# Gathers of three expert pairs in quarters, issued within the product with the third matrix, through bank g

## The chip, the core and the metric

The kernel runs on one core of one Trainium2 chip. TensorE (PE) multiplies into PSUM banks, VectorE (DVE) and ScalarE (ACT) read the banks and work on SBUF, and SyncE (SP) issues the DMAs. Each engine takes its own instructions in the order in which they stand; engines wait for each other by semaphores. The metric is the device time of one execution in microseconds, the median of several runs.

## The reference

Two layers of a backbone run for 128 context and 128 latent tokens, 256 in all, with 1024 features. What the change touches is the end of the second layer, a mixture of eight experts of which each token uses two:

```python
for e in range(N_EXPERTS):
    ye = jnp.matmul(jax.nn.silu(jnp.matmul(t, w1[e])) * jnp.matmul(t, w3[e]), w2[e])
    out = out + comb[:, e:e + 1] * ye
```

`w1` and `w3` are 1024 x 2816, `w2` is 2816 x 1024, all in 32-bit floats; `comb` is zero but for a token's two experts.

## The kernel before

**Numbers in two halves.** Every 32-bit operand is split into a high part (rounded to TensorE's fp32r) and a low part (the difference). A product is three matmuls: high x high, high x low, low x high. For weights, ScalarE casts the high part (`mwh`, line 1319) and VectorE subtracts for the low part (`mwl`, through `tt`, line 52). The tokens of an expert have `xh` and `xl`, the gated product has `gh` and `gl`.

**Pieces.** The generator `blocks` brings a weight matrix in pieces of 128 x 1024 numbers: two tiles along the contraction, 512 columns each. A piece costs one cast, one subtraction and six matmuls. Six buffers hold cast pieces (`mwh`, three in each of two pools), so a cast waits for the matmuls of the piece six places before. The loads (`mws`, `ws`, `vs`) go round a ring of larger buffers on SP's queue.

**Experts.** `experts` works through four pairs. Pair p2 holds experts 2 p2 and 2 p2 + 1. `gather` makes a selection matrix `sel` for the pair (`select`) and multiplies the 256 tokens (`hhh`, `hhl`) with it, so that each expert has its own tokens in at most 128 columns: 32 matmuls of 128 x 256 in four quarters, each quarter in one bank and two k tiles of the result; ScalarE copies `xh` from the bank (line 1387), VectorE makes `xl` (line 1388). Four transposes turn `sel` into `selT` through bank `g` (lines 1392 to 1394).

For an expert, each block of 512 columns of `w1` and `w3` gives two banks of 8 k tiles; then ScalarE applies SiLU (line 1448), VectorE multiplies, TensorE transposes the result through bank `g` (line 1452), and ScalarE and VectorE read `gh` and `gl` from there (lines 1455, 1456). The last block has 256 columns. Then the product with the third matrix, `w2`, runs in two halves of 512 columns over 22 k tiles; each half is scaled (`yh`, `yl`) and multiplied with `selT` into the accumulators `acc`.

**When the gather stands.** The first pair is gathered ahead of the experts. The others are gathered at line 1459, after the odd expert's products with `w1` and `w3` and ahead of its product with `w2`, all four quarters at once.

**PSUM.** Eight banks: three for `mm` (the products with weights, and before the change the gathers of the pairs behind the first), one for `g`, three and one for `acc`.

**The order.** The code is recorded, and a scheduler places each engine's instructions by its own estimate of when they can run, so neighbouring pieces of work interleave.

Of the kernel before, what the change touches and what calls it, by code (L numbers as in the profile page):

```python
# [7 lines left out]
F32 = mybir.dt.float32  # L8
# [4 lines left out]
ALU = mybir.AluOpType  # L13
# [11 lines left out]
KT = D // 128  # L25
# [16 lines left out]
def backbone(ctx, tc, x_prompt, x_sample, c, state_hgrn, state_mlstm_C, state_mlstm_n, state_mlstm_m,  # L42
# [5 lines left out]
    V, S, G, PE = nc.vector, nc.scalar, nc.gpsimd, nc.tensor  # L48
# [19 lines left out]
    ident = const.tile([128, 128], F32, name="ident")  # L68
# [30 lines left out]
    def bank(shape):  # L99
        return mmp.tile(shape, F32, tag="mm", name="mm", bufs=3)  # L100
# [961 lines left out]
    with ExitStack() as es:  # L1062
# [52 lines left out]
        for q4 in range(2):  # L1115
            banks = gemm_tm(ffn_w2[0], 512 * q4, 512, grhs, fbank, 1 + 3 * q4, spare)
# [33 lines left out]
    def gbank(shape):  # L1150
        return pe.tile(shape, F32, tag="g", name="g")
# [30 lines left out]
    z, _ = mix_out(1, mrhs, ms, ("e8",), obank, spare1, 2)  # L1182
# [53 lines left out]
    for tr in range(2):  # L1236
        for q4 in range(2):
            ps = bank([128, 4, 128])
# [5 lines left out]
            with tc.issue_after(last_act[0]):  # L1244
                behind = [S.copy(hh[:, tr, s], psf).ins]
# [109 lines left out]
    def experts(first_slot):  # L1355
# [5 lines left out]
        def gather(p2):  # L1361

            sel = firsts.pop() if firsts else select(p2, sl)
            xh = ms.tile([128, KT, 256], F32R, tag="e8", name="xh", bufs=2)
            xl = ms.tile([128, KT, 256], F32R, tag="e8", name="xl", bufs=2)
            rhs = [sel[:, tr].rearrange("p i t -> p (i t)") for tr in range(2)]
            def part(ps, k2, src, first, last):
                for k in range(2):
                    s = slice(128 * (k2 + k), 128 * (k2 + k) + 128)
                    for tr in range(2):  # L1370
                        mm(ps[:, k], src[:, tr, s], rhs[tr], first and k + tr == 0, last and tr == 1)

            banks = []
            if not first_slot and p2 == 0:
                banks = [pe.tile([128, 2, 256], F32, tag="acc", name="acc", bufs=3) for _ in range(3)]
                banks.append(adp.tile([128, 2, 256], F32, tag="ad", name="acc"))
                for k2, ps in zip(range(0, KT, 2), banks):
                    part(ps, k2, hh, True, False)
            for k2 in range(0, KT, 2):
                if banks:  # L1380
                    ps = banks[k2 // 2]
                else:
                    ps = bank([128, 2, 256])
                    part(ps, k2, hh, True, False)
                part(ps, k2, hl, False, True)
                o = slice(k2, k2 + 2)
                S.copy(xh[:, o], ps)
                done = V.tensor_tensor(xl[:, o], ps, xh[:, o].bitcast(F32), op=ALU.subtract).ins  # L1388
            ps = gbank([128, 2, 2, 128])
            for tr in range(2):  # L1390
                for i in range(2):
                    PE.transpose(ps[:, i, tr], sel[:, tr, i].bitcast(F32), ident)
            selT = ms.tile([128, 2, 2, 128], F32R, tag="selT", name="selT", bufs=2)
            S.copy(selT, ps)
            return sel, selT, xh, xl, done

        def slot_weights(p2, sel):
            pc = gbank([128, 2])
# [7 lines left out]

        nxt = gather(0)
        if not first_slot:
            with tc.issue_after(nxt[4]):
                V.tensor_reduce(most, pm, axis=AX.X, op=ALU.max)  # L1410
                V.tensor_copy(most_i, most)
            behind.append(nxt[4])
            late.append(nc.values_load(most_i[0:1, 0:1], min_val=0, max_val=256))
        for p2 in range(NE // 2):
            sel, selT, xh, xl, _ = nxt
            for i in range(2):
                e = 2 * p2 + i
                s = slice(128 * i, 128 * i + 128)
                gT = []
                if not first_slot and e in (2, 3):  # L1420
                    ng1 = ms.tile([128, 2, 512], F32, tag="vs", name="ng1")
                    o1 = slice(512 * (e - 2), 512 * (e - 2) + 512)
                    for j, ap in enumerate((ln1_g[1], ln1_b[1])):
                        nc.sync.dma_start(out=ng1[:, j], in_=bcast_row(ap[o1], 512))
                for f0 in range(0, DFF, 512):
                    n = min(512, DFF - f0)
                    b13 = []
                    for srcs in ([moe_w1[0, e]], [moe_w3[0, e]]) if n == 512 else ([moe_w1[0, e], moe_w3[0, e]],):
                        b = bank([128, 512])
                        for kt, wh, wl in blocks(srcs, KT, f0, n, ahead.pop(0) if ahead else ()):  # L1430
                            mm(b, xh[:, kt, s], wh, kt == 0, False)
                            mm(b, xl[:, kt, s], wh, False, False)
                            mm(b, xh[:, kt, s], wl, False, kt == KT - 1)
                        b13 += [b[:, c:c + n] for c in range(0, 512, n)]
                    if not first_slot and e == 0 and f0 == 0:
                        park(moe_w3[0, 0], (0, 2, 4, 6), 512)
                        park(moe_w1[0, 0], (0,), 1024)
                    if not first_slot and e in (2, 3) and f0 in (512, 1024):
                        tr = f0 // 1024
                        tt(x[:, tr, o1], x[:, tr, o1], ng1[:, 0], ALU.mult)  # L1440
                        tt(x[:, tr, o1], x[:, tr, o1], ng1[:, 1], ALU.add)
                    if not i and f0 == 1024:
                        if not first_slot and not p2:
                            with tc.issue_after(gated):
                                expert_weights()
                        cs = slot_weights(p2, sel)
                    t_ = wp.tile([128, n], F32, tag="wa", name="gt_", bufs=2)
                    act(t_, b13[0], AF.Silu)  # L1448
                    tt(t_, t_, b13[1], ALU.mult)
                    ps = gbank([128, n // 128, 128])  # L1450
                    for j in range(n // 128):
                        PE.transpose(ps[:, j], t_[:, j * 128:j * 128 + 128], ident)  # L1452
                    gh = ms.tile([128, n // 128, 128], F32R, tag="gh", name="gh", bufs=6)
                    gl = ms.tile([128, n // 128, 128], F32R, tag="gl", name="gl", bufs=6)
                    S.copy(gh, ps)
                    gated = V.tensor_tensor(gl, ps, gh.bitcast(F32), op=ALU.subtract).ins
                    gT += [(gh[:, j], gl[:, j]) for j in range(n // 128)]
                if i and p2 + 1 < NE // 2:
                    nxt = gather(p2 + 1)
                if e == NE - 1:  # L1460
                    out = ms.tile([128, 2, D], F32, tag="e8", name="out", bufs=2)
                for q4 in range(2):
                    o = slice(512 * q4, 512 * q4 + 512)
                    yb = bank([128, 512])
                    for kt, wh, wl in blocks([moe_w2[0, e]], 22, 512 * q4, 512):
                        gh, gl = gT[kt]
                        mm(yb, gh, wh, kt == 0, False)
                        mm(yb, gl, wh, False, False)
                        mm(yb, gh, wl, False, kt == 21)
                    if e == NE - 1 and q4:  # L1470
                        with tc.issue_after(loaded[0]):
                            gate = gate_rows(ms, "e8", 1, 1, 2)
                            ng = norm_rows(base, "p8", ln2_g[1], ln2_b[1])
                    yh = ms.tile([128, 512], F32R, tag="yh", name="yh", bufs=1)
                    yl = ms.tile([128, 512], F32R, tag="yl", name="yl", bufs=1)
                    act(yh, yb, AF.Copy, scale=cs[:, i:i + 1])
                    V.scalar_tensor_tensor(yl, yb, cs[:, i:i + 1], yh.bitcast(F32), op0=ALU.mult, op1=ALU.subtract)
                    if e == NE - 1 and q4:
                        for tr in range(2):
                            before_norm(tr, gate, out, 0)  # L1480
                    for tr in range(2):
                        new = not first_slot and e == 0
                        if new:
                            acc[tr, q4] = adp.tile([128, 512], F32, tag="ad", name="acc") if tr and q4 else abank()
                        mm(acc[tr, q4], selT[:, i, tr], yh, new, False)
                        mm(acc[tr, q4], selT[:, i, tr], yl, False, True)
# [46 lines left out]
```

## Time and profile before

| | |
|---|---|
| median of 3 runs | 1909.88 us (1909.39 to 1910.23) |
| profiled execution, its own time | 1913.11 us |
| span in its trace | 1911.4 us |
| TensorE busy | 1842.6 us, 96% |
| VectorE busy | 1473.4 us, 77% |
| ScalarE busy | 1187.9 us, 62% |
| HBM read | 493.45 MB |
| mean granted clock | 0.99 |

Durations are taken from the one profiled execution. A matmul's row tells a duration that overlaps with its neighbours; the pace is the distance from start to start. In rows of the order of time, equal instructions that follow each other are merged (x2, x4), and a bracket tells how long the engine had been idle and what ended it. The experts run from about 1085 us to the end.

### The profile page before, as it was taken

What the parts mean: (1) busy time and instruction counts of PE and PEld (TensorE: products, weight loads), DVE (VectorE), ACT (ScalarE), POOL (GpSimd) and SP (SyncE); (2) the same over time, 40 slices, a digit from 0 to 9 for tenths busy, and PEclk for the clock granted to TensorE, in tenths of its full rate; (3) what the DMA queues carried; (4) which work ended last, traced back from release to release, by engine and by line L of the source; (5) the groups of instructions that cost most, each with busy time, mean ns of one, the idle gap of its engine ahead of it and who ended that gap; (6) DMA issues with size and microseconds to landing.
All of it is one profiled execution on the core that took longest, in us unless ns stands there. A gap on an engine that the chain in (4) does not pass through costs nothing.

```text
span 1911.4 us, 30874 instructions
## 1 busy us (share of the span) xinstructions
PE 1842.6 (96%) x11846; PEld 1572.2 (82%) x11846; DVE 1473.4 (77%) x2179; ACT 1187.9 (62%) x1531; POOL 21.3 (1%) x51
## 2 busy tenths in 40 slices
PE   7999999998999899999999999999999999999996
PEld 4877889996998688788999787888887888788884
DVE  3587598676455658869957798989888898889887
ACT  4547555644444445665564587777776777677773
POOL 0000000000000000000000000000000000000000
PEclk9999999999999999999999999999999999999998
DMA  9866845567756585775555989999998999999993
GB/s 315 259 228 203 269 142 160 157 198 277 230 170 194 162 286 194 244 220 149 149 161 172 361 297 346 363 323 366 349 349 312 358 350 343 307 350 352 348 342 128
DMA packets 273579, 500.88 MB, mean 262 GB/s; under 512 B 17044, under 2 KB 56552, under 8 KB 273424
## 3 DMA queue, kind: packets, MB, share of 16 engines
q1 hardware_dynamic: 273424, 498.83, 78.0%
q8 instruction: 95, 1.56, 0.3%
q14 instruction: 60, 0.49, 0.1%
HBM read 493.45 MB, written 5.32 MB: 261 GB/s over the span
## 4 chain that ended last, share of the span: by engine, by line
PE 83%; DMA 9%; DVE 3%; ACT 2%; issue 1%; SPq 1%; DVEq 0%; ACTq 0%
PE mm L56 62%; PE fp L56 9%; DMA wa<-in_w_ada_dram 6%; PE adq L56 2%; PE pl L56 2%; PE acc L56 1%; PE pn L56 1%; DMA ws<-in_ffn_w_dram 1%; DVE wl L52 1%; PE g L1452 1%; DVE mwl L52 1%; PE pqk L56 1%; DMA ws<-in_w_in_dram 1%; PE po L56 1%; ACT wh L198 1%
## 5 line engine op out<-in xcount | busy, mean ns | idle before, releaser
L52 DVE TENSOR_TENSOR mwl<-mws,mwh 128x1024 fp32r<-128x1024 f32 x432 | 516.8, 1223 | 52.3 <-ACT mwh L1319 48.3
L1319 ACT CAST mwh<-mws 128x1024 fp32r<-128x1024 f32 x432 | 445.8, 1052 | 117.1 <-PE mm L56 109.1
L52 DVE TENSOR_TENSOR wl<-ws,wh 128x1024 fp32r<-128x1024 f32 (+1 forms) x275 | 331.4, 1207 | 189.9 <-ACT wh L198 184.8
L198 ACT CAST wh<-ws 128x1024 fp32r<-128x1024 f32 (+1 forms) x275 | 284.7, 1036 | 308.8 <-PE mm L56 149.1
L56 PE MATMUL mm<-hTh,wh 128*128 128x256 f32 x1024 | 293.8, 289 | 4.6 <-ACT wh L198 2.5
L56 PE MATMUL mm<-hTl,wh 128*128 128x256 f32 x1024 | 293.0, 287 | 1.7 <-DVE hTl L52 1.0
L56 PE MATMUL mm<-hTh,wl 128*128 128x256 f32 x1024 | 291.7, 288 | 2.4 <-DVE wl L52 2.4
L56 PE MATMUL mm<-mwh,xh 128*128 128x512 f32 x704 | 278.8, 396 | 0.0
L56 PE MATMUL mm<-mwl,xh 128*128 128x512 f32 x704 | 277.5, 399 | 0.9 <-DVE mwl L52 0.8
L56 PE MATMUL mm<-mwh,xl 128*128 128x512 f32 x704 | 278.4, 396 | 0.0
L56 PEld LDWEIGHTS mm<-hTh,wh 128*128 128x128 f32 x1024 | 196.4, 192 | 10.3 <-ACT wh L198 2.7
L56 PEld LDWEIGHTS mm<-hTh,wl 128*128 128x128 f32 x1024 | 195.3, 192 | 10.5 <-issue 5.1
L56 PEld LDWEIGHTS mm<-hTl,wh 128*128 128x128 f32 x1024 | 196.8, 192 | 8.6 <-issue 4.2
L56 PEld LDWEIGHTS mm<-mwl,xh 128*128 128x128 f32 x704 | 132.3, 188 | 32.3 <-DVE mwl L52 2.0
L56 PEld LDWEIGHTS mm<-mwh,xl 128*128 128x128 f32 x704 | 132.3, 188 | 31.8 <-DVE xl L1388 0.4
L56 PEld LDWEIGHTS mm<-mwh,xh 128*128 128x128 f32 x704 | 132.3, 188 | 30.0
L56 PE MATMUL mm<-mwh,gh 128*128 128x512 f32 x352 | 139.4, 397 | 1.5 <-ACT gt__12538 L1448 1.5
L56 PE MATMUL mm<-mwh,gl 128*128 128x512 f32 x352 | 139.4, 397 | 0.0
L56 PE MATMUL mm<-mwl,gh 128*128 128x512 f32 x352 | 138.8, 396 | 0.5 <-DVE mwl L52 0.5
L52 DVE TENSOR_TENSOR mwl<-ws,mwh 128x1024 fp32r<-128x1024 f32 x74 | 89.9, 1223 | 16.3 <-ACT mwh L1319 15.6
L56 PE MATMUL fp<-hTh,wh 128*128 128x256 f32 x352 | 100.7, 287 | 0.0
L56 PE MATMUL fp<-hTl,wh 128*128 128x256 f32 x352 | 100.1, 285 | 0.0
(600 smaller groups left out, 3119.4 us busy)
## 6 DMA issues: line engine op xcount, KB each, us to landing
mws<-in_moe_w_dram SPq DMA_DIRECT2D x202, 1024.0 KB
ws<-in_w_in_dram SPq DMA_DIRECT2D x160, 512.0 KB
wa<-in_w_ada_dram SPq DMA_DIRECT2D x96, 512.0 KB
ws<-in_moe_w_dram SPq DMA_DIRECT2D x70, 512.0 KB
ws<-in_ffn_w_dram SPq DMA_DIRECT2D x62, 512.0 KB
mws<-in_moe_w_dram SPq DMA_DIRECT2D x28, 512.0 KB
ws<-in_w_branch_a_dram SPq DMA_DIRECT2D x16, 512.0 KB
ws<-in_w_branch_b_dram SPq DMA_DIRECT2D x16, 512.0 KB
```

Source lines behind the costliest of these rows:

```text
L52: V.tensor_tensor(out, a, b, op=op)
L56: return PE.matmul(out, lhsT, rhs, start=start, stop=stop, skip_group_check=True, **kw).ins
L198: S.copy(hi, st)
L1319: S.copy(h, t_)
L1452: PE.transpose(ps[:, j], t_[:, j * 128:j * 128 + 128], ident)
```

## The change

`gather` no longer issues the quarters for the pairs behind the first. It builds `sel` and the tiles, and returns a list of five steps: four quarters, each with its copy and subtraction, and the transposes of `sel`. In the loop over the k tiles of the product with `w2`, a step is taken off the list at k tiles 4, 8, 12, 16 and 20 of the first half. The banks of these quarters come from `gbank` in place of `bank`. The first pair's steps are run at once, as before. The second pass of `experts`, behind a branch for an expert with over 128 tokens, has the same code, and all four of its pairs take a bank from `gbank`; it does not run with these inputs.

```diff
--- before.py
+++ after.py
@@ -1376,23 +1376,29 @@
                 banks.append(adp.tile([128, 2, 256], F32, tag="ad", name="acc"))
                 for k2, ps in zip(range(0, KT, 2), banks):
                     part(ps, k2, hh, True, False)
-            for k2 in range(0, KT, 2):
-                if banks:
-                    ps = banks[k2 // 2]
-                else:
-                    ps = bank([128, 2, 256])
+            def step(k2):
+                ps = banks[k2 // 2] if banks else gbank([128, 2, 256])
+                if not banks:
                     part(ps, k2, hh, True, False)
                 part(ps, k2, hl, False, True)
                 o = slice(k2, k2 + 2)
                 S.copy(xh[:, o], ps)
-                done = V.tensor_tensor(xl[:, o], ps, xh[:, o].bitcast(F32), op=ALU.subtract).ins
-            ps = gbank([128, 2, 2, 128])
-            for tr in range(2):
-                for i in range(2):
-                    PE.transpose(ps[:, i, tr], sel[:, tr, i].bitcast(F32), ident)
+                done[:] = [V.tensor_tensor(xl[:, o], ps, xh[:, o].bitcast(F32), op=ALU.subtract).ins]
+
+            def places():
+                ps = gbank([128, 2, 2, 128])
+                for tr in range(2):
+                    for i in range(2):
+                        PE.transpose(ps[:, i, tr], sel[:, tr, i].bitcast(F32), ident)
+                S.copy(selT, ps)
+
+            done = []
             selT = ms.tile([128, 2, 2, 128], F32R, tag="selT", name="selT", bufs=2)
-            S.copy(selT, ps)
-            return sel, selT, xh, xl, done
+            steps = [lambda k2=k2: step(k2) for k2 in range(0, KT, 2)] + [places]
+            if not p2:
+                while steps:
+                    steps.pop(0)()
+            return sel, selT, xh, xl, done, steps
 
         def slot_weights(p2, sel):
             pc = gbank([128, 2])
@@ -1406,13 +1412,13 @@
 
         nxt = gather(0)
         if not first_slot:
-            with tc.issue_after(nxt[4]):
+            with tc.issue_after(nxt[4][0]):
                 V.tensor_reduce(most, pm, axis=AX.X, op=ALU.max)
                 V.tensor_copy(most_i, most)
-            behind.append(nxt[4])
+            behind.append(nxt[4][0])
             late.append(nc.values_load(most_i[0:1, 0:1], min_val=0, max_val=256))
         for p2 in range(NE // 2):
-            sel, selT, xh, xl, _ = nxt
+            sel, selT, xh, xl, _, steps = nxt
             for i in range(2):
                 e = 2 * p2 + i
                 s = slice(128 * i, 128 * i + 128)
@@ -1457,12 +1463,15 @@
                     gT += [(gh[:, j], gl[:, j]) for j in range(n // 128)]
                 if i and p2 + 1 < NE // 2:
                     nxt = gather(p2 + 1)
+                    steps = nxt[5]
                 if e == NE - 1:
                     out = ms.tile([128, 2, D], F32, tag="e8", name="out", bufs=2)
                 for q4 in range(2):
                     o = slice(512 * q4, 512 * q4 + 512)
                     yb = bank([128, 512])
                     for kt, wh, wl in blocks([moe_w2[0, e]], 22, 512 * q4, 512):
+                        if steps and kt and kt % 4 == 0:
+                            steps.pop(0)()
                         gh, gl = gT[kt]
                         mm(yb, gh, wh, kt == 0, False)
                         mm(yb, gl, wh, False, False)
```

TensorE at the gather of the third pair, before. The names: `sel` with `hhh` and `hhl` is the gather, `g<-ident,gt` transposes the gated product, `mwh,gh` is the product with the third matrix.

```order
L56 MATMUL mm<-mwl,xh 128x512
L56 MATMUL mm<-sel,hhh 128x256 x4
L56 MATMUL mm<-sel,hhl 128x256 x4
L56 MATMUL mm<-sel,hhh 128x256 x4
L56 MATMUL mm<-sel,hhl 128x256 x4
L1452 MATMUL g<-ident,gt__15194 128x128 x2
L56 MATMUL mm<-mwh,gh 128x512
```

TensorE at the second quarter of the same pair, in the changed kernel:

```order
L56 MATMUL mm<-mwl,gh 128x512
L56 MATMUL g<-sel,hhh 128x256 x4
L56 MATMUL g<-sel,hhl 128x256 x4
L56 MATMUL mm<-mwl,gh 128x512
L56 MATMUL mm<-mwh,gh 128x512
```

The third and fourth quarter, which stood back to back ahead of the product with the third matrix, now stand apart within it, in bank g.

ScalarE around the same gather, before. `gh` reads the transposes of the gated product, `mwh` are the casts of weight pieces, `xh` the copies of the gather.

```order
L1455 CAST gh<-g 128x512
L1319 CAST mwh<-ws 128x1024
L1319 CAST mwh<-mws 128x1024 x2
L1387 CAST xh<-mm 128x512 x2
L1448 ACTIVATE gt__15194<-mm 128x256
L1319 CAST mwh<-ws 128x1024
L1387 CAST xh<-mm 128x512 x2
L1455 CAST gh<-g 128x256
```

ScalarE in the changed kernel, from the same last `gh` on:

```order
L1461 CAST gh<-g 128x256
L1319 CAST mwh<-mws 128x1024 x2
L1319 CAST mwh<-vs 128x1024
L1319 CAST mwh<-mws 128x1024 x2
L1385 CAST xh<-g 128x512
L1319 CAST mwh<-mws 128x1024 x4
L1485 ACTIVATE yh<-mm,cs 128x512
L1319 CAST mwh<-mws 128x1024
L1385 CAST xh<-g 128x512
```

The four copies of `xh` come singly now, each with four to five casts of weight pieces between it and the next, and the first five casts behind the last `gh`.

## Rows read from the trace of the kernel before

**Rows 1.** The page's slices, 40 equal parts of the span: TensorE's busy tenths.

```profile
PE   7999999998999899999999999999999999999996
```

**Rows 2.** Stretches in us: length, busy us (instructions) by engine, clock, DMA.

```profile
core 0: us, PE busy (x) PEld busy (x) DVE busy (x) ACT busy (x) POOL busy (x), PEclk, DMA share, GB/s
1185.00:1251.00 66.00, 66.00 (x293) 53.34 (x292) 60.02 (x56) 52.21 (x56) 0.00 (x0) 1.00 1.02 363
...
1458.23:1461.62 3.39, 3.39 (x17) 3.39 (x17) 2.66 (x4) 0.59 (x1) 0.00 (x0) 0.54 1.04 372
...
1662.44:1665.79 3.35, 3.35 (x16) 3.35 (x17) 3.35 (x5) 1.24 (x2) 0.00 (x0) 0.55 1.03 390
```

**Rows 3.** What TensorE waited for, 1240 to 1870 us: total, times, longest.

```profile
PE mm L56 <- DVE xl L1388: 7.3, 2, 3.6
PE mm L56 <- DVE mwl L52: 0.8, 2, 0.5
PE g L1452 <- DVE gt__15031 L52: 0.4, 1, 0.4
```

**Rows 4.** Order of time, third pair: start us, duration us, engine, line, operation.

```profile
1451.35 0.59 ACT L1455 CAST gh<-g 128x512 fp32r<-128x512 f32 x1 [3.49 <-PE g L1452]
...
1452.99 1.05 ACT L1319 CAST mwh<-ws 128x1024 fp32r<-128x1024 f32 x1 [1.05 <-PE mm L56]
...
1453.94 1.99 ACT L1319 CAST mwh<-mws 128x1024 fp32r<-128x1024 f32 x2
...
1454.19 0.40 PE L56 MATMUL mm<-mwl,xh 128*128 128x512 f32 x1
...
1455.83 1.06 ACT L1387 CAST xh<-mm 128x512 fp32r<-128x512 f32 x2
...
1457.48 1.28 DVE L1388 TENSOR_TENSOR xl<-mm,xh 128x512 fp32r<-128x512 f32 x2
...
1458.23 1.22 PE L56 MATMUL mm<-sel,hhh 128*128 128x256 f32 x4 [3.64 <-DVE xl L1388]
...
1461.62 0.38 PE L1452 MATMUL g<-ident,gt__15194 128*128 128x128 f32 x2
...
1461.76 0.48 PE L56 MATMUL mm<-mwh,gh 128*128 128x512 f32 x1
```

**Rows 5.** Order of time, fourth pair.

```profile
1654.94 0.60 PE L1452 MATMUL g<-ident,gt__16875 128*128 128x128 f32 x4
...
1655.58 0.59 ACT L1455 CAST gh<-g 128x512 fp32r<-128x512 f32 x1 [5.80 <-PE g L1452]
...
1657.15 2.36 DVE L52 TENSOR_TENSOR mwl<-mws,mwh 128x1024 fp32r<-128x1024 f32 x2 [0.26 <-ACT mwh L1319]
...
1658.42 0.40 PE L56 MATMUL mm<-mwl,xh 128*128 128x512 f32 x1
...
1662.44 0.99 PE L56 MATMUL mm<-sel,hhh 128*128 128x256 f32 x4 [3.62 <-DVE xl L1388]
...
1665.79 0.56 PE L1452 MATMUL g<-ident,gt__16934 128*128 128x128 f32 x2
...
1666.43 0.40 PE L56 MATMUL mm<-mwh,gl 128*128 128x512 f32 x1
...
1666.66 0.40 PE L56 MATMUL mm<-mwl,gh 128*128 128x512 f32 x1
```

**Rows 6.** Order of time, second pair, TensorE.

```profile
1252.88 0.63 PE L56 MATMUL mm<-sel,hhl 128*128 128x256 f32 x4
...
1253.81 0.63 PE L56 MATMUL mm<-sel,hhl 128*128 128x256 f32 x4
...
1254.62 0.74 PE L56 MATMUL mm<-sel,hhh 128*128 128x256 f32 x4 [0.19 <-DVE gt__13440 L52]
...
1255.20 0.64 PE L56 MATMUL mm<-sel,hhl 128*128 128x256 f32 x4
```

**Rows 7.** DMA of the stretch 1085 to 1870 us.

```profile
DMA packets 143936, 268.04 MB, mean 341 GB/s; under 512 B 5133, under 2 KB 21517, under 8 KB 143886
```

## The prediction, made before the changed kernel ran

> **What bounds the kernel now.** I began with the page's slices [rows 1]: from the 24th on, where the experts run, TensorE is busy nine tenths or more in every slice but the last. A table of stretches sharpens this [rows 2]: between 1185 and 1251 us TensorE is busy all 66.00 us, VectorE 60.02 and ScalarE 52.21, at 363 GB/s. So TensorE sets the pace there, and VectorE runs at 91% beside it. The list of what TensorE waited for between 1240 and 1870 us is short [rows 3]: 7.3 us in two waits for xl, the low half of the gathered tokens; then 0.8 us in two for weight pieces and 0.4 in one at the bank g. No DMA heads it.
>
> The two xl waits are the gathers of the third and fourth pair. The order in time shows how one arises [rows 4]. ScalarE has stood 3.49 us for the transposes of the gated product and reads them at 1451.35. Then it casts three pieces (one at 1452.99, two from 1453.94) before it reaches xh at 1455.83, and VectorE reaches xl at 1457.48. TensorE's next work is the third quarter of the gather, which needs one of the three mm banks, and that is free only once xl is made. Its last product before the wait starts at 1454.19 and takes 0.23 us of pace, so it stands from 1454.42 to 1458.23: 3.81 us. The product with the third matrix stands behind the waiting quarter, and its pieces are cast meanwhile. Then comes a second loss: from 1458.23 to 1461.62 the granted clock averages 0.54 [rows 2], so most of the sixteen gather products run at 1.2 GHz in place of 2.4. The fourth pair repeats both [rows 5]: its last product starts at 1658.42, so it is idle from 1658.65 to 1662.44, 3.79 us, and then has a stretch at 0.55.
>
> **What the change removes.** Full pace for gather products is read from the second pair, where eight of them take from 1252.88 to 1253.81 [rows 6]: 0.93 us, so sixteen take 1.86.
> Third pair: idle 3.81, and half clock 3.39 - 1.86 = 1.53.
> Fourth pair: idle 3.79, and half clock 3.35 - 1.86 = 1.49. Two transposes and the first product behind them are slow too: 0.64 us (1665.79 to 1666.43) against 0.14 + 0.23 in the third pair, where the clock is back (1461.62 to 1461.76) [rows 4, 5]; 0.27 more.
> Second pair: the clock does not drop, but its third quarter starts at 1254.62 where 1253.81 + 0.47 would do, 0.34 us late, and its first four products take 0.58 in place of 0.47, 0.11 more [rows 6].
> Together 3.81 + 1.53 + 3.79 + 1.76 + 0.45 = 11.3 us, if nothing new waits.
>
> **What it adds and moves.** Nothing is computed more or less: a pair keeps 32 products and four transposes on TensorE, four casts and four subtractions behind them. SP issues the same DMAs; of two ws loads that stood together some now have a larger load between them. No wait of TensorE for a DMA stands in [rows 3], so I take zero for that, with rival C as its other end. The moved parts have three prices.
>
> First, each quarter now goes through the single bank g, so a quarter may wait for the xl of the one before, and the first for the gl of the last transposes. In the new order 22 to 34 other products lie between two quarters (three pairs), 5.1 to 7.8 us. ScalarE's cast of a quarter stands about five pieces further on in its queue than the quarter on TensorE. There are six buffers for cast pieces, so when the quarter ends ScalarE is at most one cast of about 1.05 us short of it. Then 0.6 for xh, VectorE's 1.2 for the piece ahead (two take 2.36 in [rows 5]), 0.7 for xl: some 3.5 us after the quarter, before 5.1 have passed. I take zero; what hides it is the product with the third matrix. Without that cover a quarter pays at least its own emptying, which I estimate at 0.59 + 0.69 = 1.28 us from the halves of the paired rows of xh (1.06) and xl (1.28) and a little for the hand-over.
>
> Second, ScalarE's wait for the gated product's transposes does not go away. Of the last full column block, in the new order they stand 2.7 pieces ahead of the first piece that ScalarE has not cast by then in the third pair, and 1.7 in the fourth. That piece is late next. With the rows of the fourth pair, counted from the transposes at 1654.94: gh begins 0.64 later, VectorE starts on the piece at 2.21 (1657.15) and ends it at 3.4. TensorE wants its low half after the transposes (0.36), 1.7 pieces of six products (2.35) and two products more (0.47), at 3.2. So 0.2 to 0.3 us of wait in the fourth pair; in the third it is wanted at 4.6, no wait. VectorE then gains about 0.2 us a piece. In the experts behind, the new order has three places with 2.0 pieces between; there it is wanted at 3.6, nearly level. I put 0.8 us for all of these. The bounds: nothing, since the old order shows 0.8 us of waits for pieces in all [rows 3]; and the two waits of 3.8 come back whole, which is rival A.
>
> Third, the last quarter is issued late, in the fourth pair two pieces into the next expert's first product, which needs its xl for the seventh of eight k tiles. Counted from the end of that product's first piece, VectorE is done after some 3.6 us, and TensorE wants it after 1.4 (second piece) + 0.93 (the quarter) + 1.4 (third) + 0.23 = 4.0. Close but covered: zero, at most 0.5.
>
> Sum: 11.3 - 0.8 = 10.5 us. The profiled execution took 1913.11 us, its span 1911.4 and 1.7 around it; so 1902.6 in its terms. It lay 3.2 us above the median of the three runs, 1909.88, and from that median I forecast 1899.4 us. Lowest: all 11.3 and the 1.2 of other waits gone, 1897.4, and about 1 us for the measurement.
>
> **The rivals.** A. The stall moves. Its root in the rows is ScalarE's wait for the transposes (3.49 us, and 5.80 in the fourth pair [rows 5]), not the gather. If TensorE waits for a low piece where it waited for xl, the idle comes back: half of it gives about 1905, all of it with the clock 1909. For it: the new order keeps these waits of ScalarE and brings more like them in the later experts. Against it: counted in the old orders, TensorE stood with two pieces of the next product already cast in the third pair, and without the gather it would have gone on; my count leaves 1 us of room there.
>
> B. Slower: one bank for everything. If ScalarE or VectorE come to the quarters late, TensorE waits at each with the weight products behind it. Twelve quarters at 1.28 us are 15.4 us, which gives 1899.4 + 15.4 = 1914.8. It decides from 11.3 / 12 = 0.94 us a quarter. Against it: transposes pass through g all along, and in 630 us TensorE waited once there, 0.4 us, for its input and not for the bank [rows 3].
> The Trainium skill (Perfetto Trace Analysis, Matmuls) says that independent groups of products should rotate through different PSUM banks, so that ScalarE and VectorE empty one while the next is filled; the change does the reverse with the quarters. By that rule the 15.4 us would be paid. The trace does not decide it: rotation over three banks did not spare the 7.3 us, and no row has gather products in a single bank.
>
> C. No gain: weights cannot come faster. From 1085 to 1870 us 268.04 MB move, at 341 GB/s [rows 7]; 11 us less needs 268.04 / 774 = 346. The 363 GB/s over 66 us [rows 2] speaks against it. It would leave the time near 1909.
>
> **How the numbers follow.** Forecast 0.73 (its own range 1896.5 to 1903), A 0.15, B 0.08, C 0.04. The range of 8 in 10 goes into A: 1896 to 1907. A measurement of this kernel tells 0.2% from no change, so faster means under 1906.1: the forecast and a third of A, 0.78. The same is the rest of A and C, 0.14. Slower is B, 0.08.
>
> **What would show it.** Right: in the list of TensorE's waits the line for xl is gone or under 1 us; the granted clock is 1.00 in every stretch from 1085 us to the end of the last expert; each quarter of eight products takes about 0.93 us; ScalarE still waits for the transposes of the gated product, without TensorE standing. A: waits of TensorE for low pieces, of 1 us and more, just behind the transposes of the last full column block. B: a dozen waits of products into g for xl. C: casts that wait for a DMA.

## The result, and the profile after

The changed kernel takes 1903.03 us, the median of five runs (1901.91 to 1904.31), against 1910.23 for five runs of the kernel before (1909.39 to 1916.76). The ratio is 0.9948, with a 95% interval of 0.9931 to 0.9965: faster by about half a per cent. Its profiled execution took 1904.31 us with a span of 1902.6, against 1913.11 and 1911.4.

TensorE's waits between 1240 and 1862 us in the changed kernel, the stretch that answers to 1240 to 1870 in [rows 3], by engine, what was waited for, total, times and longest:

```profile
PE mm L56 <- DVE mwl L52: 2.1, 5, 0.6
PE g L1458 <- DVE gt__15031 L52: 0.4, 1, 0.4
```

Against [rows 3], the 7.3 us for xl are gone, and the waits for low pieces have grown from 0.8 to 2.1 us. (One more, of 0.5 us, stands behind both stretches, at 1880.38 before and at 1871.61 in the changed kernel.) No quarter waits at bank g.

The stretches of the third and fourth pair in the changed kernel (columns as in [rows 2]):

```profile
1435.00:1490.00 55.00, 54.52 (x254) 44.62 (x253) 50.21 (x49) 39.20 (x46) 0.00 (x0) 1.00 0.98 349
1640.00:1700.00 60.00, 59.90 (x279) 48.77 (x278) 51.02 (x51) 42.75 (x51) 0.00 (x0) 1.00 0.99 359
```

The granted clock, 0.54 and 0.55 behind the stalls in [rows 2], is 1.00 in both, and 1.00 on average from 1085 to 1885 us. The order in time of the third pair, against [rows 4]:

```profile
1449.71 0.60 PE L1458 MATMUL g<-ident,gt__15135 128*128 128x128 f32 x4
...
1450.35 0.59 ACT L1461 CAST gh<-g 128x512 fp32r<-128x512 f32 x1 [3.51 <-PE g L1458]
...
1452.48 0.40 PE L56 MATMUL mm<-mwh,gh 128*128 128x512 f32 x1
...
1461.09 0.64 PE L56 MATMUL g<-sel,hhh 128*128 128x256 f32 x4
1461.56 0.63 PE L56 MATMUL g<-sel,hhl 128*128 128x256 f32 x4
...
1469.49 0.63 PE L56 MATMUL g<-sel,hhh 128*128 128x256 f32 x4
```

ScalarE still stands 3.5 us for the transposes, as before. But at 1452.48, 2.8 us after the transposes, TensorE is in the product with the third matrix, and the first quarter comes 8.6 us later, at 1461.09, and runs at full pace: four products in 0.47 us, as in [rows 6]. No bracket stands behind its rows: it waited for nothing.

To compare executions without what happens ahead of the experts, I take the time from the start of the first weight product of the experts to the start of the last. In the changed kernel these rows are:

```profile
1089.56 0.66 PE L56 MATMUL mm<-mwh,xh 128*128 128x512 f32 x2
...
1884.55 0.40 PE L56 MATMUL mm<-mwl,gh 128*128 128x512 f32 x1
```

794.99 us. In the kernel before the same two start at 1089.17 and 1893.31: 804.14 us. The change gains 9.15 us here. Following every 66th product through both traces tells where: 0.5 us at the second pair, 5.4 at the third, 5.1 at the fourth, 10.9 in all; then 1.8 us are given back in the last two experts.

One thing shows without a run. Take the kernel before and change one word, `bank` to `gbank` where the gather takes its bank, without the steps and the loop: the order of its instructions on TensorE, VectorE, ScalarE and SyncE is the same as the changed kernel's. So with bank g the steps at k tiles 4 to 20, the most visible part of the diff, place nothing; the scheduler spreads the quarters as soon as their bank is g. As built, the change is its bank.

### The profile page after: what moved, and what is told of

Same layout as the page of the kernel before. It is cut to its first block, busy times and chain, and to the rows that moved or that the text cites. A ratio compares the mean times of both kernels' runs of the same rounds, so it can differ in the third digit from the quotient of the medians.

```text
span 1902.6 us, 30784 instructions
## 1 busy us (share of the span) xinstructions
PE 1841.9 (97%) x11846; PEld 1570.5 (83%) x11846; DVE 1466.1 (77%) x2179; ACT 1177.5 (62%) x1531; POOL 21.2 (1%) x51
## 4 chain that ended last, share of the span: by engine, by line
PE 85%; DMA 9%; DVE 3%; ACT 1%; issue 1%; SPq 1%; DVEq 0%; ACTq 0%
PE mm L56 63%; PE fp L56 9%; DMA wa<-in_w_ada_dram 6%; PE adq L56 2%; PE pl L56 2%; PE acc L56 1%; PE g L56 1%; PE pn L56 1%; DVE mwl L52 1%; PE g L1458 1%; DMA ws<-in_w_in_dram 1%; DVE wl L52 1%; DMA ws<-in_ffn_w_dram 1%; PE pqk L56 1%; PE po L56 1%
## 5 line engine op out<-in xcount | busy, mean ns | idle before, releaser
L1319 ACT CAST mwh<-mws 128x1024 fp32r<-128x1024 f32 x432 | 437.4, 1051 | 83.0 <-PE mm L56 75.8
L56 PE MATMUL fp<-hTh,wl 128*128 128x256 f32 x352 | 100.2, 285 | 0.0
```

The source lines that it names most:

```text
L56: return PE.matmul(out, lhsT, rhs, start=start, stop=stop, skip_group_check=True, **kw).ins
L1319: S.copy(h, t_)
```

## The experiments

All times between the first and the last weight product are the rows above, read in each run's own trace. Each ratio is against runs of the kernel before that were made beside it: their median is 1914.32 us for e0, e1, e5 and e6, and 1912.63 for e7, e11 and e12. The times in the expectations go by about 1910 us for the kernel before, so it is the ratio that can be compared.

| run | first weight product starts | last starts | between | against before |
|---|---|---|---|---|
| before | 1089.17 | 1893.31 | 804.14 | |
| the change | 1089.56 | 1884.55 | 794.99 | -9.15 |
| before again (e0) | 1091.86 | 1896.11 | 804.25 | +0.11 |
| quarters in mm (e1) | 1092.90 | 1888.76 | 795.86 | -8.28 |
| third quarter in g (e5) | 1094.42 | 1898.64 | 804.22 | +0.08 |
| last two in g (e6) | 1092.44 | 1898.78 | 806.34 | +2.20 |
| last three in g (e7) | 1094.20 | 1889.19 | 794.99 | -9.15 |
| four in g, one behind the other (e11) | 1086.46 | 1916.02 | 829.56 | +25.42 |
| g in the third pair alone (e12) | 1088.28 | 1887.07 | 798.79 | -5.35 |

**e0, the kernel before again.**

> The kernel before, unchanged, profiled once more, since its profiled execution lay 3.2 us above its median. If that belongs to the stalls (the clock drops in some executions and not in others), the new profile's idle at the third and fourth pair is again about 3.6 us each and the time follows the number of drops, 1.5 us each. If it lies elsewhere, the experts take the same time as in the first profile to within 0.5 us and the difference stands ahead of them.

Median 1915.39 us, the ratio to its own kind 1.0013 (0.9999 to 1.0026). Between the weight products it took 804.25 us, 0.11 more than in the first profile, with the same two waits of 3.6 us; but the first weight product started 2.69 us later. So what differs between these two executions lies ahead of the experts. Over the nine traces that start lies between 1086.46 and 1094.42 us, and the change touches nothing there. A median of five runs carries this scatter; the column "between" does not.

**e1, the change with the quarters in mm.**

```diff
-                ps = banks[k2 // 2] if banks else gbank([128, 2, 256])
+                ps = banks[k2 // 2] if banks else bank([128, 2, 256])
```

> The changed kernel with its quarters back in the three mm banks; the steps stay in the product with the third matrix. In its order the third quarter of the third and fourth pair stands four to five pieces behind the transposes it used to follow, with pieces of the third product ahead of it. Theory (the stall is the third quarter standing ahead of that product while its bank is busy): the two waits for xl are gone here too, 1902 to 1905 us, ratio to before 0.994 to 0.997. Rival (the bank g is what does it): the waits of 3.6 us and the half clock come back, 1908 to 1911 us.

1905.12 us, ratio 0.9954 (0.9938 to 0.997). TensorE's waits from 1075 us on:

```profile
PE mm L56 <- DVE mwl L52: 3.0, 7, 0.6
PE mm L56 <- ACT gt__12538 L1454: 1.5, 1, 1.5
PE g L1458 <- DVE gt__15031 L52: 0.4, 1, 0.4
```

No line for xl. Bank g is not needed for the gain: here the steps in the loop do what the bank did. The first quarter of the third pair starts at 1456.21, behind the first matmul of the third product at 1455.74, so that product has its mm bank before any quarter takes one. The gain is 0.9 us smaller, with one more wait for a low piece (0.48 us at 1530.22) and one of the transposes ahead of it (0.31).

**e5, the third quarter alone in g.**

```diff
-                    ps = bank([128, 2, 256])
+                    ps = gbank([128, 2, 256]) if k2 == 4 else bank([128, 2, 256])
```

> The kernel before, with only the third quarter of each later pair in bank g; the others stay in mm and in their place. In its order the fourth quarter now stands where the third stood and takes the bank that the third took. Theory (a quarter ahead of the third product waits for a bank that xl frees): two waits of about 3.6 us for xl and both drops of the clock remain, 1908 to 1911 us. Rival (four banks for four quarters are enough): no wait, about 1900.

1913.09 us, ratio 0.9996 (0.9982 to 1.001), and 7.3 us in two waits for xl as before. Four banks do not help while the next user of mm stands ahead of the product.

**e6, the last two quarters in g.** As e5 with `k2 > 2`.

> The kernel before, with the third and fourth quarter of each later pair in bank g and the first two in mm. In its order the first two stay ahead of the third product and the last two stand some eight pieces into it; the order of the later experts is the old one. Theory: no wait for xl, clock 1.00, and none of the new waits for low pieces that the changed kernel has in its last two experts: 1898 to 1901 us, 1 to 3 us below the changed kernel. Rival (the new waits belong to the gather, not to the order of the later experts): like the changed kernel, 1902 to 1904.

1913.44 us, ratio 0.9992 (0.9976 to 1.0008): my theory failed, and so did its rival. Only the first two quarters stand ahead of the third product, and the stall is there whole:

```profile
1457.38 0.40 PE L56 MATMUL mm<-mwl,xh 128*128 128x512 f32 x1
...
1459.03 1.06 ACT L1387 CAST xh<-mm 128x512 fp32r<-128x512 f32 x2
...
1460.69 1.28 DVE L1388 TENSOR_TENSOR xl<-mm,xh 128x512 fp32r<-128x512 f32 x2
...
1461.42 0.80 PE L56 MATMUL mm<-mwh,gh 128*128 128x512 f32 x1 [3.64 <-DVE xl L1388]
```

Now the product itself (`mwh,gh`) waits 3.64 us for xl. Its sum needs an mm bank as well, and two of the three hold quarters; it starts when the first xl is made. It is 2.2 us slower than before. Behind the stall the weight products start 0.43 us apart in place of 0.23, and the stretch from 1461.40 to 1469.00 has a mean granted clock of 0.59 over 7.6 us:

```profile
1461.40:1469.00 7.60, 7.58 (x21) 5.97 (x21) 4.48 (x5) 2.59 (x3) 0.00 (x0) 0.59 0.76 279
```

**e7, the first quarter in mm, three in g.** As e5 with `k2 > 0`. The theory was mended for it: not a waiting quarter, but whatever next needs an mm bank.

> The kernel before, with the first quarter of each later pair in mm and the other three in bank g. In its order the first quarter stands ahead of the third product, the others 8 to 23 pieces into it. Theory as the runs so far leave it (what stalls is the next user of an mm bank, be it a quarter or the third product, when two of the three banks hold quarters whose xl stands behind three casts): with one quarter in mm a bank is left for the product, no wait for xl, 8 to 10 us less between the first weight product and the last than before. Rival (any quarter ahead of the product stalls it): the waits of 3.6 us remain and the gain is under 2 us.

1901.78 us, ratio 0.9934 (0.9908 to 0.996), 9.15 us less between the products, as much as the change. Its waits from 1240 us on:

```profile
PE mm L56 <- DVE mwl L52: 2.6, 6, 0.6
PE g L1452 <- DVE gt__15031 L52: 0.4, 1, 0.4
```

One quarter ahead of the product is harmless. Two stall it where ScalarE reaches their copies late. The second pair shows the other case: in the kernel before it too has its quarters in mm, but there ScalarE copies the first one right behind gh, with no cast of a weight piece between, and the wait behind is 0.19 us [rows 6], not 3.6:

```profile
1253.16 0.58 ACT L1455 CAST gh<-g 128x512 fp32r<-128x512 f32 x1
1253.63 0.60 ACT L1387 CAST xh<-mm 128x512 fp32r<-128x512 f32 x1
```

**e11, four quarters in g, nothing between.** The product's first matmul is held until the last quarter is issued; the rest as the kernel before.

```diff
...
-                    ps = bank([128, 2, 256])
+                    ps = gbank([128, 2, 256])
...
-                        mm(yb, gh, wh, kt == 0, False)
+                        with tc.issue_after(ahead_of.pop()) if ahead_of else nullcontext():
+                            mm(yb, gh, wh, kt == 0, False)
```

> The kernel before, with all quarters of the later pairs in bank g and the third product held back until the last quarter is issued, so that the four quarters follow each other on TensorE with nothing between. This is what the rule on rotating banks speaks of. Theory (bank g costs nothing only because the product fills the time of emptying): each quarter but the last waits for xh and xl of its own bank, 1.3 to 1.5 us, three a pair, besides the backlog of casts and the clock; 10 to 25 us longer than before. Rival (one bank is no price at all): the same time as before or less.

1939.96 us, ratio 1.0145 (1.0119 to 1.0171), 25.4 us more between the products, just over the 10 to 25 expected. Its waits, and one quarter's emptying with the start of the next:

```profile
PE g L56 <- DVE xl L1388: 12.6, 9, 1.4
PE g L1454 <- DVE gl L1458: 8.2, 3, 2.9
PE g L56 <- DVE gl L1458: 2.8, 3, 0.9
```

```profile
1467.67 0.59 ACT L1387 CAST xh<-g 128x512 fp32r<-128x512 f32 x1 [2.61 <-PE g L56]
1468.28 0.69 DVE L1388 TENSOR_TENSOR xl<-g,xh 128x512 fp32r<-128x512 f32 x1 [2.77 <-ACT xh L1387]
...
1469.03 1.22 PE L56 MATMUL g<-sel,hhh 128*128 128x256 f32 x4 [1.40 <-DVE xl L1388]
```

Each quarter but the first waits 1.40 us for the emptying of the one before (0.59 + 0.69 and the hand-over), nine times. The other 11.0 us of waits are of the last transposes and of each pair's first quarter, for the gl that empties the same bank ahead of them. The clock falls with the waits: 0.64 between 1461 and 1478 us. The Trainium skill (Perfetto Trace Analysis, Matmuls) says that independent groups should rotate through different PSUM banks, so that the emptying of one overlaps the matmuls of the next; with one bank and nothing between, nothing overlaps, and the trace agrees with it. In the change the same single bank costs nothing: 22 to 34 weight products lie between two quarters of a pair, and no quarter waits.

**e12, bank g in the third pair alone.** As e5 with `p2 == 2`.

> The kernel before, with bank g for the quarters of the third pair alone. Two things are told apart. Gain: the wait of 3.6 us and the half clock of the third pair are gone, 5.3 us, and those of the fourth remain. New waits: if they come from the order that follows a gather without a stall, then the last two experts, which here follow the old gather of the fourth pair, have none of the waits of 0.4 to 0.7 us for low pieces (1742, 1827 and 1849 us in the changed kernel); if they belong to the loads or to ScalarE and VectorE in these experts as such, they are there. Sum between the first weight product and the last: 5 us less than before.

1907.33 us, ratio 0.9977 (0.9962 to 0.9993); 5.35 us less between the products, and the one wait of 3.6 us that is left is the fourth pair's. TensorE's waits from 1700 us on, of e12 and then of the changed kernel:

```profile
PE acc L56 <- ACT yh L1476: 0.8, 1, 0.8
PE mm L56 <- DVE mwl L52: 0.5, 1, 0.5
```

```profile
PE mm L56 <- DVE mwl L52: 1.8, 4, 0.6
```

The one wait for a low piece in e12, 0.5 us at 1874.13, is among the four of the changed kernel and stands in the kernel before too. The other three, at 1742.56, 1828.36 and 1849.57, are new: 1.25 us in this list, and 1.8 counted from start to start. They are absent in e12, while e1 and e7, with other gathers, have all three. So they go with a fourth pair that does not stall, and equally with the new order of the last two experts, which e1 and e7 share with the changed kernel, while e6 and e12 have the old one there. How one arises in the changed kernel:

```profile
1824.13 2.00 ACT L1319 CAST mwh<-mws 128x1024 fp32r<-128x1024 f32 x2
1825.36 1.22 DVE L52 TENSOR_TENSOR mwl<-ws,mwh 128x1024 fp32r<-128x1024 f32 x1
...
1826.49 0.68 DVE L1462 TENSOR_TENSOR gl<-g,gh 128x512 fp32r<-128x512 f32 x1
1827.09 2.35 DVE L52 TENSOR_TENSOR mwl<-mws,mwh 128x1024 fp32r<-128x1024 f32 x2
...
1828.36 0.50 PE L56 MATMUL mm<-mwl,xh 128*128 128x512 f32 x1 [0.56 <-DVE mwl L52]
```

VectorE makes gl between two pieces, and the piece that TensorE needs was cast by 1825.2 but is only begun at 1827.09. In the old order VectorE has the same piece ahead of that gl, here and at 1742.56, so for these two the new order is at least part of the cause. Whether they would arise in that order behind a stall too was not separated, since e12 has both the old order there and the stall.

## Why the prediction came out as it did

**What went.** The idle and the half clock were sized from rows at 0.45 us for the second pair, 5.34 for the third and 5.55 for the fourth. The traces give 0.5, 5.4 and 5.1. The fourth is short by the small wait that was counted for it, about 0.3 us behind 1651.55; the last 0.2 is not assigned. That the clock's loss goes with the idle is shown by the clock of 1.00 and by e6, where it came back with the stall.

**Bank g.** Taken at zero, and it is zero: no wait of a quarter. Rival B, with 1.28 us a quarter, did not come; e11 shows that its mechanism is real and its price 1.40 us, where the cover is taken away. The prediction named the cover rightly.

**The new waits.** This term was mis-sized: 0.8 us for all of them, of which 0.2 to 0.3 in the fourth pair. Measured, about 0.3 there and 1.8 us in the last two experts, 2.1 in all. I looked for them at places where transposes leave ScalarE few pieces; they came where VectorE has gl or the gated product between two pieces, in the last two experts. With 10.5 us forecast and 9.15 measured between the products, this term is nearly all of the difference of 1.35.

**Rival A.** The stall did not move. ScalarE's wait for the transposes of the gated product stayed, and grew from 26.9 us in 11 waits (1240 to 1870 us) to this (1240 to 1862):

```profile
ACT gh L1461 <- PE g L1458: 50.7, 25, 4.9
```

TensorE did not stand for it. So the wait that starts the chain is not what costs; what costs is that mm banks are held until their copies come, behind three casts.

**Rival C.** No wait for a DMA stands in the list. The experts from 1085 to 1862 us ran at 345 GB/s, close to the 346 that this rival held too fast, and the fourth pair's stretch at 359.

**What the account had wrong.** It said that the third quarter, standing ahead of the product, is what stalls it. e6 took that quarter away, and the product stalled itself. The statement that covers both, and e7 and the second pair as well: with two quarters in mm whose copies come late, the next user of an mm bank waits for xl. The forecast survived because the change takes all quarters out of mm; in that it was lucky, for by its account taking the third and fourth out would have done, and e6 shows that it doesn't.

**The time.** 1899.4 was forecast from a median of 1909.88; 1903.03 was measured beside 1910.23. That is at the upper edge of the forecast's own range (1896.5 to 1903) and inside the range of 8 in 10. Of the 3.6 us, 1.3 are missing between the products, mostly the new waits. The rest lies within what executions differ by ahead of the experts, 8 us between the extremes of nine traces; no run attributes it further.

## What to carry to other kernels

A wait's releaser tells which buffer was late, not which instruction would have been better elsewhere: before moving the one that waited, ask who takes the same bank next. In this kernel a single bank was no price where other work filled the emptying, and one of 1.4 us each time where nothing did; the order shows which. Where a scheduler places the code, compare the built orders of each part of a change first: here one word gave the order of the whole diff.

## What was not expected

The same stall of 3.8 us cost different amounts behind it. In the kernel before the clock was back when the product began at 1461.76 [rows 4], 3.5 us after the wait; in e6 the products were still at half pace (0.43 us) 5 us after it, at 1466.28. The other traces bear this out. The 8 us from the end of the wait, third pair before, then third and fourth pair of e6 (columns as in [rows 2]):

```profile
1458.23:1466.23 8.00, 8.00 (x37) 7.18 (x38) 5.49 (x8) 3.79 (x6) 0.00 (x0) 0.80 0.76 278
1461.42:1469.42 8.00, 8.00 (x22) 6.30 (x23) 4.46 (x5) 3.01 (x3) 0.00 (x0) 0.61 0.72 264
1667.01:1675.01 8.00, 8.00 (x25) 6.35 (x26) 5.79 (x7) 3.93 (x5) 0.00 (x0) 0.66 0.92 336
```

At all seven stalls with gather products right behind them (two each in before, e0 and e5, one in e12) the clock of these 8 us is 0.79 or 0.80, and at both of e6, with the third product behind them, 0.61 and 0.66. This speaks for the work behind the stall and against the execution, as far as two stalls of one trace can; why is open. At e6's clocks 3.1 and 2.7 us of the 8 are lost, against 1.6 to 1.7, and the 2.5 us between them are about the 2.2 by which e6 is slower than before.

And executions of the same program differ by several us ahead of the experts, while the 804 us of the experts repeat to 0.1 us: a small change in one stage is measured better from stage marks in two traces than from medians of whole executions.
